# Eleven 512-column matmuls of a live operand with ones between the products of the up and the down projection of a hybrid decoder layer

## The chip, the cores and the metric

The kernel runs on one core of one Trainium2 chip. The metric is the device time of one execution in microseconds, the median of several runs. Beside it there is one execution taken by the hardware profiler; every row of a view comes from that one.

## The reference, cut to what matters

One decoder layer, float32, 512 tokens of 2048 channels. It has an adaptive normalisation, two attention branches with gates, and then a feed-forward part with a causal three-tap convolution:

```python
x = x + gt_a * parallel_mixers(h, ...)
h = rms_norm(x, g_ffn[l]) * (1.0 + sc_f) + sh_f
x = x + gt_f * conv_ffn(h, w_up[l], w_conv[l], b_conv[l], w_down[l])

def conv_ffn(h, w_up, w_conv, b_conv, w_down):
    u = h @ w_up                                    # 512 x 2048 by 2048 x 11264
    up = jnp.pad(u, ((0, 0), (CONV_W - 1, 0), (0, 0)))
    conv = b_conv
    for j in range(CONV_W):
        conv = conv + w_conv[j] * up[:, j:j + S]
    gate, val = jnp.split(conv, 2, axis=-1)         # 5632 each
    return (jax.nn.silu(gate) * val) @ w_down       # 5632 x 2048
```

The change touches only the two matrix products of `conv_ffn`.

## The kernel before, in words

Every float32 product is made of three matmuls: each operand is split into a high part (a rounded copy, made by ScalarE) and a low part (the rest, made by VectorE), and high·high, high·low and low·high are accumulated in PSUM. Weights arrive by DMA on SyncE's queue in the tile `raw` and are split into `whl`; activations lie in `slot` tiles of 128 x 512.

Before the feed-forward part, most matmuls have 512 columns (`mm3`, lines 188 to 190). The last of these, in `up_group(0)`, make the first 8 column tiles of the up projection and end at about 1321.5 us of the profiled execution.

The rest of the up projection and all of the down projection go through `seven`. It takes a list of `Pair`s. A pair makes two 128-row output tiles (for all 512 tokens) from a 2 x 2 block product done with seven block products in place of eight (a Strassen-like scheme): `p1, p7, p6, p2, p5, p4, p3`, each with its own evacuation `e1 ... e3`. One block product is `K` contraction tiles by three matmuls of 256 columns (lines 1256 to 1258). It goes to X (the left half of the pair's first bank `bx`), Y or Z (the halves of its second bank `by`). Four bank pairs go round (`all_banks`), so pair n uses the banks that pair n-4 used. The second bank of a pair is first written by `p7`, its second product, and is read last in `e4`, after its sixth.

`work_up` has 40 pairs with K = 8 (168 matmuls each; the tile of the gate half and of the value half of `w_up`). `work` has 32 pairs in four chunks c of 8, with K = `DH[c]` = 5, 6, 6, 5 (105, 126, 126 and 105 matmuls a pair). The chunks add into `x1_d`, and the last one writes the output.

`run` goes through the products in order. For each it first prepares the weights of the product `AHEAD` further on: VectorE makes sums and differences of weight blocks in place (`comb`, line 1133), and `hilo` splits the result (line 175 on ScalarE, 176 on VectorE; `tc.issue_after(left[0].ins)` keeps that split behind the last evacuation). Then it issues the product's matmuls and its evacuation (`copy`, lines 1137 and 1139, ScalarE; `plus`, lines 1143 and 1145, VectorE). A hook per product does side work: in the up projection it makes early sums, in the down projection it loads (line 1754) and splits the operands of the next chunk. Those operands, made from the f tiles in DRAM, are kept in `held_by[c]` until the chunk's last pair. `h2[0][0]` is the high part of the first contraction tile of h; it is an operand of all 40 up pairs.

The order on each engine is that of the program, sorted by priorities and a planner's estimated times, with `issue_after` where it is set by hand.

Two lines elsewhere put 512-column matmuls with the all-ones tile `ones_r` as weights into the stream. They are in `flush_cols`, which spreads sums over the partitions, and fall now and then between the 256-column matmuls of an earlier use of `seven` (the gate columns, 583 to 743 us):

```python
PE.matmul(b, ones_r, hi, start=True, stop=False)    # line 937
PE.matmul(b, ones_r, lo, start=False, stop=True)    # line 938
```

Of the kernel before, what the change touches and what calls it, by code (L numbers as in the profile page):

```python
# [21 lines left out]
KD = D // P  # L22
# [9 lines left out]
def trunk_layer_kernel(  # L32
# [21 lines left out]
    DH=(5, 6, 6, 5),  # L54
# [6 lines left out]
    V, A, G, PE, SP = nc.vector, nc.scalar, nc.gpsimd, nc.tensor, nc.sync  # L61
# [14 lines left out]
    def get(dt=F32):  # L76

        i = min(free, key=lambda n: rested[n])
        free.remove(i)
        if cur[i] is None or cur[i].dtype != dt:  # L80
            cur[i] = pool.tile([P, T], dt, name=f"slot{i}", tag=f"slot{i}")
        held[id(cur[i])] = i
        return cur[i]
# [4 lines left out]
    def put(*ts, lag=2):  # L88

        for t in ts:  # L90
            i = held.pop(id(t))
            rested[i] = clock[0] + lag
            free.append(i)
# [4 lines left out]
    ones_r = pool.tile([P, P], F32R, name="ones_r")  # L98
# [46 lines left out]
    last = {}  # L145
# [767 lines left out]
    done = [0]  # L913
# [167 lines left out]
    KH = KD // 2  # L1081
# [8 lines left out]
    def operands(act, ts):  # L1090
        return (quarter(act, 0, 0), quarter(act, KH, 0), quarter(act, KH, HT)) + tuple(sums(ts, n) for n in range(4))
# [8 lines left out]
    class Pair:  # L1100


        def __init__(self, rs, load, fin, K=KH, scale=None, onto=None):
            self.rs, self.load, self.fin, self.K, self.scale, self.onto = rs, load, fin, K, scale, onto

    def seven(work, pairs_of_banks, hook=None, AHEAD=2, ring=None):

# [129 lines left out]
        def prepare(q):  # L1237
            if q < len(steps):
                ready[q] = steps[q][0]()
# [5 lines left out]
        def run(then=None):  # L1245
            for q, (_, o, r, ev, first, K) in enumerate(steps):
                prepare(q + AHEAD)
                if then:
                    then(q - len(steps))
                wh, wl = ready.pop(q)  # L1250
                assert len(r) == K
                for k in range(K):
                    ks = slice(k * P, (k + 1) * P)
                    rh, rl = r[k]
                    last = k == K - 1
                    PE.matmul(o, wh[:, ks], rh, start=first and k == 0, stop=False, skip_group_check=True)  # L1256
                    PE.matmul(o, wh[:, ks], rl, start=False, stop=False, skip_group_check=True)  # L1257
                    PE.matmul(o, wl[:, ks], rh, start=False, stop=last, skip_group_check=True)  # L1258
                ev()
                clock[0] += 1  # L1260
                if hook:
                    hook(q, len(steps))
# [7 lines left out]
    for i in range(KH // 2):  # L1270
        raw = [get() for _ in range(4)]
        ta, tb_ = get(), get()
        for j in range(2):
            k, o = 2 * i + j, slice(j * HT, (j + 1) * HT)
# [10 lines left out]
    def gate_out(i):  # L1285
        def fin(u1, u2):
            G.dma_start(gate_d[G0 + 2 * i], u1)
            G.dma_start(gate_d[G0 + 2 * i + 1], u2)
            put(u1, u2)
        return fin  # L1290
# [10 lines left out]
    def gate_hook(q, n):  # L1301
        gate_tick()
        if q == n - 7:
            reload_mq()

    rs = operands(h, h_sums)
    start, run = seven([Pair(rs, lambda blk, i=i: w_gs[i, blk], gate_out(i)) for i in range((31 - G0) // 2)],
          ((MM[0], MM[1]), (MM[2], MM[3])), gate_hook)
# [257 lines left out]
    h2 = []  # L1566
# [3 lines left out]
    for tb in range(4):  # L1570
        spread = PE.matmul(rb[:, tb * P:(tb + 1) * P], rstd2[:, tb:tb + 1].to_broadcast([P, P]), ident,
                           start=True, stop=True)
# [27 lines left out]
    NF_ = DFF // P  # L1600
# [3 lines left out]
    KINDS = ("r11", "t3", "t2", "r21", "t1", "t4", "r22")  # L1604
# [74 lines left out]
    def f_tile(i, u1, u2, give):  # L1679
        j = 4 + i  # L1680
        g = conv(j, u1)
        A.activation(g, g, AF.Silu)
        v = conv(44 + j, u2)
        give((u1, u2))
        V.tensor_tensor(v, v, g, ALU.mult)
        f_out(j, v)
        put(g)
# [4 lines left out]
    def ffn_out(i):  # L1692
        def fin(u1, u2):
            for n, ds, _ in late:
                if n == i:
                    G.dma_start(ds[0], u1)
                    G.dma_start(ds[1], u2)
                    ring.extend((u1, u2))
                    return
            f_tile(i, u1, u2, ring.extend)  # L1700
        return fin
# [41 lines left out]
    held_by = [{n: [] for n in KINDS} for _ in DH]  # L1743
# [69 lines left out]

    all_banks = [(bank[2 * i], bank[2 * i + 1]) for i in range(4)]
    rs = operands(h2, tsum)
    work_up = [Pair(rs, lambda blk, i=i: w_ups[i, blk], ffn_out(i)) for i in range(NF_ - 4)]

    def down_pair(c, j):
        ns = (2 * j, 2 * j + 1)
        x1 = []  # L1820

        def load(blk):
            if c == len(DH) - 1 and not x1:
                for n in ns:
                    x1.append(get())
                    G.dma_start(x1[-1], x1_d[n])
            return w_downs[c][j, blk]

        def fin(*us):
            for i, (n, u) in enumerate(zip(ns, us)):  # L1830
                if x1:
                    V.tensor_tensor(u, u, x1[i], ALU.add)
                    G.dma_start(out[n * P:(n + 1) * P, :], u)
                else:
                    G.dma_start(x1_d[n], u, accum_op=ALU.add)
            ring.extend(us)
            put(*x1)

        o = ops[c]
        return Pair(tuple(o[n] for n in ("r11", "r21", "r22", "t1", "t2", "t3", "t4")), load, fin, K=DH[c],  # L1840
                    scale=tuple(mod[:, 80 + n:81 + n] for n in ns),
                    onto=(lambda i: (out[ns[i] * P:(ns[i] + 1) * P, :], x1[i]))
                    if c == len(DH) - 1 and j == KD // 2 - 1 else None)

    ring = deque(get() for _ in range(4))
    up_start, up_run = seven(work_up, all_banks, up_hook, ring=ring)
    work = [down_pair(c, j) for c in range(len(DH)) for j in range(KD // 2)]

    def hook(q, n):
        c, r = divmod(q, 56)  # L1850
        if r >= 49:
            put(*held_by[c][KINDS[r - 49]])
        ahead(q + 1, c + 1)
        late_tiles(q)
# [73 lines left out]
```

## Time and profile before

| | |
|---|---|
| three runs | 2515.29, 2515.98, 2541.91 us; median 2515.98 |
| profiled execution, its own time | 2519.35 us |
| its span, first to last instruction | 2517.3 us |
| granted TensorE clock over the span | 0.999 |
| busy: TensorE matmul / VectorE / ScalarE / GpSimd | 99% / 86% / 51% / 15% |

The profiled execution has 2.05 us outside its span, and is 3.4 us above the median of the runs.

In the views, PE is a TensorE matmul, PEld a weight load, DVE VectorE, ACT ScalarE, POOL GpSimd, SP SyncE. Matmuls overlap in the pipeline, and their ends are modelled: a 256-column matmul is shown as 276 ns long though the next one starts earlier. So the time that a matmul takes from the stream is the distance from its start to the next start, not its duration. A view by windows counts each instruction that touches the window. In a row of the timeline the columns are start (us), duration (us), engine, line, operation, output<-input, shapes, count and, in brackets, the idle time before it and what ended it.

### The profile page before, as it was taken

How to read it: one execution, taken by the hardware profiler on the slowest of the kernel's cores; microseconds unless marked ns; L12 is line 12 of the kernel's file. 1: busy time of each engine (PE TensorE's matmuls, PEld its weight loads, DVE VectorE, ACT ScalarE, POOL GpSimd, SP SyncE). 2: the span in 40 equal slices, each digit the busy share in tenths (PEclk: the TensorE clock that was granted, in tenths of full speed). 3: DMA queues.
4: the chain of work that ended last, by engine and by line, in shares of the span. 5: the costliest groups of instructions: out<-in, count | busy, mean ns of one | idle time of the engine just before them, and what ended most of it. 6: DMA issues, size and time to landing. Idle time of an engine off the chain costs nothing.

```text
span 2517.3 us, 45148 instructions
## 1 busy us (share of the span) xinstructions
PE 2500.6 (99%) x17328; PEld 2281.1 (91%) x17328; DVE 2168.0 (86%) x3484; ACT 1283.2 (51%) x2039; POOL 374.1 (15%) x671
## 2 busy tenths in 40 slices
PE   9999999999999999999999999999999999999999
PEld 8887688889998778888889999999999999999999
DVE  6976997788878767977879999999999998989988
ACT  6564444444445445323445555555555555666654
POOL 1000011110023224200101000000011024414120
PEclk9999999999999999999999999999999999999999
DMA  9953146555685479976524343343344458878673
GB/s 363 390 156 98 49 146 191 180 164 180 202 275 172 147 233 349 304 266 211 190 76 153 124 150 130 126 154 129 127 153 151 131 170 235 233 170 233 164 210 124
DMA packets 216444, 466.41 MB, mean 185 GB/s; under 512 B 23930, under 2 KB 65556, under 8 KB 216228
## 3 DMA queue, kind: packets, MB, share of 16 engines
q1 hardware_dynamic: 170404, 344.93, 42.1%
q0 software_dynamic: 45792, 118.59, 15.5%
q8 instruction: 135, 2.21, 0.4%
q14 instruction: 81, 0.66, 0.1%
q10 hardware_dynamic: 32, 0.01, 0.0%
HBM read 398.16 MB, written 65.27 MB: 184 GB/s over the span
## 4 chain that ended last, share of the span: by engine, by line
PE 80%; issue 10%; DMA 4%; DVE 3%; POOL 1%; ACT 1%; SPq 0%; POOLq 0%; DVEq 0%; ACTq 0%
PE bank L1256 16%; PE bank L1258 16%; PE bank L1257 15%; PE bank L188 8%; PE bank L189 8%; PE bank L190 8%; PE bank L419 2%; DMA slot<-in_w_ada 2%; PE bank L420 2%; PE bank L421 2%; DMA raw<-in_w_ada 1%; PE bank L655 1%; PE bank L1404 1%; DMA slot<-f 1%; PE bank L844 1%
## 5 line engine op out<-in xcount | busy, mean ns | idle before, releaser
L1256 PE MATMUL bank<-slot,whl 128*128 128x256 f32 x3920 | 1080.7, 277 | 4.9 <-ACT slot L1137 2.3
L1257 PE MATMUL bank<-slot,whl 128*128 128x256 f32 x3920 | 1079.2, 276 | 0.0
L1258 PE MATMUL bank<-slot,whl 128*128 128x256 f32 x3920 | 1068.8, 277 | 1.9 <-DVE whl L176 1.8
L1256 PEld LDWEIGHTS bank<-slot,whl 128*128 128x128 f32 x3920 | 735.8, 188 | 8.1 <-ACT slot L1137 3.7
L1257 PEld LDWEIGHTS bank<-slot,whl 128*128 128x128 f32 x3920 | 735.9, 188 | 0.2
L1258 PEld LDWEIGHTS bank<-slot,whl 128*128 128x128 f32 x3920 | 729.8, 188 | 2.9 <-DVE whl L176 2.9
L175 ACT ACTIVATE whl<-raw 128x1024 fp32r<-128x1024 f32 (+2 forms) x560 | 531.4, 950 | 349.8 <-PE bank L1257 177.3
L176 DVE TENSOR_TENSOR whl<-raw,whl 128x1024 fp32r<-128x1024 f32 (+2 forms) x560 | 607.9, 1088 | 86.7 <-ACT whl L175 83.6
L1133 DVE TENSOR_TENSOR raw<-raw 128x1024 f32<-128x1024 f32 (+2 forms) x320 | 347.6, 1086 | 5.4 <-DMA raw<-in_w_ups 3.1
L167 ACT ACTIVATE whl<-raw 128x1024 fp32r<-128x1024 f32 (+4 forms) x182 | 187.4, 1034 | 294.7 <-PE bank L190 152.9
L168 DVE TENSOR_TENSOR whl<-raw,whl 128x1024 fp32r<-128x1024 f32 (+4 forms) x182 | 216.3, 1190 | 88.5 <-ACT whl L167 86.4
L189 PE MATMUL bank<-slot,whl 128*128 128x512 f32 x592 | 234.9, 397 | 0.0
L188 PE MATMUL bank<-slot,whl 128*128 128x512 f32 x592 | 232.2, 400 | 0.7 <-ACT slot L1586 0.7
L188 PE MATMUL bank<-whl,slot 128*128 128x512 f32 (+2 forms) x608 | 230.6, 382 | 0.7 <-DVE slot L1368 0.7
L190 PE MATMUL bank<-whl,slot 128*128 128x512 f32 (+2 forms) x608 | 230.8, 380 | 0.0
L189 PE MATMUL bank<-whl,slot 128*128 128x512 f32 (+2 forms) x608 | 230.3, 379 | 0.0
L190 PE MATMUL bank<-slot,whl 128*128 128x512 f32 x592 | 229.9, 397 | 0.0
L889 DVE SCALAR_TENSOR_TENSOR slot<-slot,c_act,slot 128x512 f32<-128x512 f32 x203 | 151.4, 748 | 23.8 <-DMA slot<-in_w_ada 22.0
L1139 ACT ACTIVATE slot<-bank 128x256 f32<-128x256 f32 x192 | 73.5, 383 | 174.8 <-PE bank L1258 174.6
L188 PEld LDWEIGHTS bank<-whl,slot 128*128 128x128 f32 x608 | 114.1, 188 | 22.6 <-issue 2.8
L188 PEld LDWEIGHTS bank<-slot,whl 128*128 128x128 f32 x592 | 111.2, 188 | 25.4 <-issue 1.7
L189 PEld LDWEIGHTS bank<-slot,whl 128*128 128x128 f32 x592 | 111.3, 188 | 24.3 <-issue 1.2
(315 smaller groups left out, 3165.0 us busy)
## 6 DMA issues: line engine op xcount, KB each, us to landing
slot<-in_w_ada SPq DMA_DIRECT2D x344, 256.0 KB, 5.0
raw<-in_w_ups SPq DMA_DIRECT2D x160, 512.0 KB, 3.6
raw<-in_w_in SPq DMA_DIRECT2D x50, 512.0 KB, 3.5
raw<-in_w_down SPq DMA_DIRECT2D x64, 384.0 KB, 4.3
raw<-in_w_down SPq DMA_DIRECT2D x64, 320.0 KB, 4.5
slot<-f POOLq DMA_DIRECT2D x154, 128.0 KB, 4.9
f<-slot POOLq DMA_DIRECT2D x66, 256.0 KB, 5.3
raw<-in_w_gs SPq DMA_DIRECT2D x32, 512.0 KB, 4.2
```

The lines of the kernel that those rows point to most:

```text
L167: A.activation(hi, raw[:, :w], AF.Copy)
L168: last["lo"] = V.tensor_tensor(lo, raw[:, :w], r32(hi), ALU.subtract)
L175: return (A.activation(dst_hi, src, AF.Copy), V.tensor_tensor(dst_lo, src, r32(dst_hi), ALU.subtract))
L176: V.tensor_tensor(dst_lo, src, r32(dst_hi), ALU.subtract))
L188: PE.matmul(o, lh, rh, start=first, stop=False)
L189: PE.matmul(o, lh, rl, start=False, stop=False)
L190: PE.matmul(o, ll, rh, start=False, stop=last)
L889: V.scalar_tensor_tensor(acc, ts[i], c_act[:, k:k + 1], acc, op0=ALU.mult, op1=ALU.add)
L1133: V.tensor_tensor(o[:, :W], a[:, :W], b[:, :W], op)
L1256: PE.matmul(o, wh[:, ks], rh, start=first and k == 0, stop=False, skip_group_check=True)
L1257: PE.matmul(o, wh[:, ks], rl, start=False, stop=False, skip_group_check=True)
L1258: PE.matmul(o, wl[:, ks], rh, start=False, stop=last, skip_group_check=True)
```

## The change

`Pair` takes one more argument, `wide`. Where a pair has it, `run` issues one more matmul ahead of the pair's first product: weights `ones_r` (128 x 128 ones), moving operand a 128 x 512 high-part tile that is live at that time, output the whole second bank of the pair, which holds nothing needed then; `p7` starts it anew later. Nothing reads the result. It is pinned behind the last matmul of the product before. Pairs 2, 4 and 20 of the up projection have it (operand `h2[0][0]`), and pairs 1 and 5 of each of the four chunks of the down projection (operand: the first tile kept for the chunk): 3 + 8 = 11.

```diff
-        def __init__(self, rs, load, fin, K=KH, scale=None, onto=None):
+        def __init__(self, rs, load, fin, K=KH, scale=None, onto=None, wide=None):
...
                 wh, wl = ready.pop(q)
                 assert len(r) == K
+                if q % 7 == 0 and work[q // 7].wide:
+                    with tc.issue_after(done.ins):
+                        PE.matmul(pairs_of_banks[q // 7 % len(pairs_of_banks)][1], ones_r, work[q // 7].wide(), start=True, stop=True)
...
-                    PE.matmul(o, wl[:, ks], rh, start=False, stop=last, skip_group_check=True)
+                    done = PE.matmul(o, wl[:, ks], rh, start=False, stop=last, skip_group_check=True)
...
-    work_up = [Pair(rs, lambda blk, i=i: w_ups[i, blk], ffn_out(i)) for i in range(NF_ - 4)]
+    work_up = [Pair(rs, lambda blk, i=i: w_ups[i, blk], ffn_out(i), wide=(lambda: h2[0][0]) if i in (2, 4, 20) else None)
+               for i in range(NF_ - 4)]
...
-                    if c == len(DH) - 1 and j == KD // 2 - 1 else None)
+                    if c == len(DH) - 1 and j == KD // 2 - 1 else None,
+                    wide=(lambda: held_by[c][KINDS[0]][0]) if j in (1, 5) else None)
```

More of the change, by code (lines that the diff above doesn't have):

```diff
@@ L1100, in trunk_layer_kernel @@
     class Pair:
-        def __init__(self, rs, load, fin, K=KH, scale=None, onto=None):
-            self.rs, self.load, self.fin, self.K, self.scale, self.onto = rs, load, fin, K, scale, onto
+        def __init__(self, rs, load, fin, K=KH, scale=None, onto=None, wide=None):
+            self.rs, self.load, self.fin, self.K, self.scale, self.onto, self.wide = rs, load, fin, K, scale, onto, wide
     def seven(work, pairs_of_banks, hook=None, AHEAD=2, ring=None):
```

## Prediction

> **What bounds the kernel now.** I read the page first: busy shares, clock, chain and the costliest groups.
>
> ```profile
> span 2517.3 us, 45148 instructions
> PE 2500.6 (99%) x17328; PEld 2281.1 (91%) x17328; DVE 2168.0 (86%) x3484; ACT 1283.2 (51%) x2039; POOL 374.1 (15%) x671
> ...
> PEclk9999999999999999999999999999999999999999
> ...
> PE 80%; issue 10%; DMA 4%; DVE 3%; POOL 1%; ACT 1%; SPq 0%; POOLq 0%; DVEq 0%; ACTq 0%
> ...
> L1256 PE MATMUL bank<-slot,whl 128*128 128x256 f32 x3920 | 1080.7, 277 | 4.9 <-ACT slot L1137 2.3
> ```
>
> TensorE is busy throughout and makes 80% of the chain that ended last. The time is that of its stream of matmuls, so anything added to the stream counts unless it falls into a wait.
>
> Next, the stages of the changed part by windows on PE. The matmul counts give the limits: 40 up pairs of 168, then chunks of 8 pairs of 105, 126, 126 and 105. (A count runs one or two over, for instructions that only touch the window.)
>
> ```profile
> core 0: us, PE busy (x), PEclk, DMA share, GB/s
> 1321.54:2084.85 763.31, 762.59 (x6721) 1.00 0.43 144
> 2084.85:2184.71 99.86, 97.34 (x842) 1.00 0.80 216
> 2184.71:2304.02 119.31, 118.36 (x1010) 1.00 0.75 202
> 2304.02:2418.75 114.73, 114.65 (x1010) 1.00 0.76 197
> 2418.75:2514.20 95.45, 95.38 (x842) 1.00 0.47 155
> ```
>
> Chunks 1 and 2 do the same work, but chunk 1 takes 4.6 us longer; chunk 0 takes 4.4 us longer than chunk 3. To see why, I put windows without any wait side by side (same columns).
>
> ```profile
> 1340.00:1425.00 85.00, 85.00 (x752) 1.00 0.42 140
> 2205.00:2290.00 85.00, 85.00 (x724) 1.00 0.65 166
> 638.00:651.00 13.00, 13.00 (x113) 1.00 0.58 189
> 655.00:668.00 13.00, 13.00 (x117) 1.00 0.60 207
> ```
>
> All are fully busy at granted clock 1.00, and yet there are **two paces** of the same 256-column matmul. The last one juts out of the window by up to 0.28 us, so 85.28/752 = 113.4 ns and 85.28/724 = 117.8 ns. The difference, 4.4 ns, lasts as long as nothing interrupts the stream. The slow pace begins here at a wait and ends at another:
>
> ```profile
> 2203.04 0.28 PE L1258 MATMUL bank<-slot,whl 128*128 128x256 f32 x1
> 2203.83 0.39 PE L1256 MATMUL bank<-slot,whl 128*128 128x256 f32 x1 [0.51 <-ACT slot L1137]
> 2204.05 0.28 PE L1257 MATMUL bank<-slot,whl 128*128 128x256 f32 x1
> ...
> 2292.85 0.28 PE L1258 MATMUL bank<-slot,whl 128*128 128x256 f32 x1
> 2293.57 0.39 PE L1256 MATMUL bank<-slot,whl 128*128 128x256 f32 x1 [0.43 <-ACT whl L175]
> ```
>
> So 88.8 us at 117.8 ns, 754 matmuls, cost 754 x 4.4 ns = 3.3 us; that is most of chunk 1's excess. Chunk 0's excess is waits.
>
> The other runs matter here. 2541.91 is 26 us above its neighbours. The up projection has next to no waits (762.59 busy of 763.31, and 6720 x 113.4 ns is 762.0), so a pace once taken can last through it; at the slow one its 6,720 matmuls would cost 30 us more. That fits, but no row shows that run.
>
> **The change part by part.** It adds eleven matmuls of 512 columns with weights `ones_r`, and removes or moves nothing. VectorE, ScalarE, GpSimd and the DMA queues issue nothing new. The trace has this very operation between products: `flush_cols` in the gate columns.
>
> ```profile
> 651.35 0.28 PE L1257 MATMUL bank<-slot,whl 128*128 128x256 f32 x1
> 651.47 0.39 PE L937 MATMUL bank<-slot,ones_r 128*128 128x512 f32 x1
> 651.70 0.28 PE L1258 MATMUL bank<-slot,whl 128*128 128x256 f32 x1
> 651.81 0.28 PE L1256 MATMUL bank<-slot,whl 128*128 128x256 f32 x1
> 651.93 0.28 PE L1257 MATMUL bank<-slot,whl 128*128 128x256 f32 x1
> ...
> 654.08 0.28 PE L1258 MATMUL bank<-slot,whl 128*128 128x256 f32 x1
> 654.19 0.40 PE L938 MATMUL bank<-slot,ones_r 128*128 128x512 f32 x1
> 654.43 0.28 PE L1256 MATMUL bank<-slot,whl 128*128 128x256 f32 x1
> 654.55 0.28 PE L1257 MATMUL bank<-slot,whl 128*128 128x256 f32 x1
> 654.67 0.28 PE L1258 MATMUL bank<-slot,whl 128*128 128x256 f32 x1
> 654.78 0.28 PE L1256 MATMUL bank<-slot,whl 128*128 128x256 f32 x1
> 654.89 0.28 PE L1257 MATMUL bank<-slot,whl 128*128 128x256 f32 x1
> ```
>
> *Price in the quick pace.* From 654.08 to 654.89, 0.81 us, there are five 256-column steps at 113.4 ns, 0.567; the rest, **0.24 us**, is the wide one with the slight irregularity behind it. Its weights load beside the matmul before, as with every other.
>
> *Effect on the pace.* The window 638 to 651 ran at 13.28/113 = 117.5 ns, and 655 to 668 at 13.28/117 = 113.5 ns; the switch is at the wide matmul at 651.47. The one at 654.19 came in the quick pace and left it so. A wide matmul between products thus ends the slow pace, and I think this is what the change would do if it does anything.
>
> The sum, against the profiled execution's 2519.35 us:
> - *Up projection, pairs 2, 4 and 20* (a pair is 168 x 113.4 ns = 19.05 us, so about 1361, 1399 and 1704 us): no wait absorbs them there; 3 x 0.24 = +0.72.
> - *Down, chunk 2 pair 5, chunk 3 pairs 1 and 5*: these chunks run almost without a wait; with chunk 2 pair 1, which is near the last small one, 4 x 0.24 = +0.96.
> - *Chunk 0 pairs 1 and 5, chunk 1 pair 1*: waits of PE follow within a pair or two:
>
> ```profile
> PE bank L1256 <- ACT slot L1137: 2.3, 4, 0.8
> PE bank L1256 <- ACT whl L175: 1.0, 3, 0.4
> ```
>
>  These (2084 to 2320 us) are for ScalarE's split of a weight block or the evacuation ahead of it. If their end is set by ScalarE and VectorE, the added time falls into them: between 0 and 3 x 0.24 = 0.72. I take 0, since the waits total 3.3 us.
> - *Chunk 1 pair 5* (about 2259): +0.24, and it ends the slow pace 34 us before 2292.85: 34/0.1178 = 288 matmuls x 4.4 ns = -1.27. The wait at 2292.85 may take that back: -1.0 to +0.24.
>
> Sum: 0.72 + 0.96 + (0 to 0.72) + (-1.0 to +0.24) = +0.7 to +2.6 us. The profiled execution is 3.4 us above the median of the runs, about one slow stretch. So I take it that the median run has no such stretch, hence no gain in chunk 1 (and its pair 5 goes into the wait at 2293 like its pair 1), and get 2515.98 + 1.7 = **2517.7 us**. With the ends it is 2516.7 to 2518.6.
>
> *Waits added.* The wide matmul needs its bank read out, by the pair four earlier, three pairs ago: 57 us in the up projection, 36 us in the shorter chunks. Only pair 2 follows other work; the last read of those banks is
>
> ```profile
> L1597 DVE SCALAR_TENSOR_TENSOR slot<-bank,wcv,slot x4: 741/745/745, 1320.3 to 1329.4; 128x510 f32<-128x510 f32 x4
> ```
>
>  and ends at 1330.2, 31 us before. The operands were read by an earlier pair. If it did wait, everything on PE would stand behind it, one for one.
>
> A place where the Trainium skill speaks against the change: "TensorE: Matmul & The Clock Gate", section "Back-to-back issue gap", gives a warm gap of N/2.4 + 2.5 ns, which is 109 ns at 256 columns and 216 at 512. By that page there is one pace only, nothing to switch, and the eleven cost an estimated 2.4 us in full. The trace agrees on neither figure: 113.4 and 117.8 ns at granted clock 1.00, and 0.24 us for the wide one.
>
> **Rivals.**
>
> *A slow stretch is cured.* If usual runs do have slow stretches like that in chunk 1, and waits don't take the time back, up to 3.3 us go for 1.7 spent: 2514.4. For it: 2204 to 2292 recurs if the waits there are the same each time. Against: pair 1 of chunk 1 comes just ahead of that wait, so the nearest cure comes 55 us after it.
>
> *The wide matmul leaves PE in the slow pace* (slower). Behind a run of 512-column matmuls the stream did start slow:
>
> ```profile
> 1321.32 0.39 PE L190 MATMUL bank<-slot,whl 128*128 128x512 f32 x1
> 1321.55 0.28 PE L1256 MATMUL bank<-slot,whl 128*128 128x256 f32 x1
> 1321.66 0.28 PE L1257 MATMUL bank<-slot,whl 128*128 128x256 f32 x1
> 1321.78 0.28 PE L1258 MATMUL bank<-slot,whl 128*128 128x256 f32 x1
> 1321.90 0.28 PE L1256 MATMUL bank<-slot,whl 128*128 128x256 f32 x1
> ```
>
>  Three steps in 0.35 us are 117 ns. If one lone wide matmul did this too, all of the up projection from 1361 on (724 us, 6,380 matmuls, 28 us) and chunks 2 and 3 from 2318 (196 us, 1,730, 7.6 us) would be slow: 2515.98 + 2.6 + 35.6 = 2554. If only that at pair 20 did, (2085 - 1704)/0.1134 x 4.4 ns = 14.8: 2532. It decides at the first one, at 1361. Against it: both insertions above ended in the quick pace.
>
> *The order shifts.* Eleven more instructions change the planner's times, and splits or evacuations on ScalarE and VectorE can come in another order in chunks 0 to 2. The waits of 3.3 us go or double, and a wait may start a slow stretch of 3.3 us: 2511 to 2524.
>
> *It does nothing that counts*: all eleven lie in waits or are dropped: 2516.0. Against it: there are no waits at seven of the places.
>
> **How the numbers follow.** Forecast 0.58, a cured stretch 0.13, slow pace left behind 0.08, order shifted 0.16, nothing 0.05. The range is 2511 to 2526: it takes the forecast, the cure, nothing and the shifted order, with 2 us above for a slow stretch in more than one place; it leaves out the slow pace left behind. A measurement of this kernel tells a difference of about 1%, 25 us, from no change. No case reaches 25 us below (0.02 for what I don't see); above it are the slow pace in full and a start in it that no wide matmul ends (0.06); same 0.92.
>
> **What the profile after would show.** Eleven matmuls of 128x512 at a new line in `run`, none with idle time before it, each 0.24 us to the next start. 1340 to 1425 has 752 matmuls less some three; a window from 1710 to 2080 keeps 113.4 ns. Chunk 2 and 3 are 0.5 us longer each, chunk 0 and 1 may be shorter or longer by their waits. If the pace is 113.4 ns in every window behind a wide matmul, the reading of the pace is right. If a window after one is at 117.8 ns, it is wrong, and so is the price. If a run like that of 2541.91 starts the up projection slow, the wide matmul at 1361 ends it, and the run costs at most 336 matmuls x 4.4 ns = 1.5 us more: the runs after should lie closer together. A forecast 10 us off would mean that the order of the splits has moved: seen as new waits of PE for lines 175, 176 or 1137 in the up projection, where there are none now.

## The result, and the profile after

Twenty-two runs each: the kernel after has a median of 2519.06 us (2514.37 to 2527.11), the kernel before 2542.95 us (2513.21 to 2549.70). The ratio of the mean times is 0.9942, 95% interval 0.9915 to 0.9969: about half a per cent faster; the medians lie 24 us apart, 0.9%. (Single runs of 3,000 us and more, two of before and three of the kernels tried further below, are left out throughout.)

The medians hide what happened. The times of before fall into **two groups**, 8 of 22 at 2513 to 2519 us (median 2515.6) and 14 of 22 at 2542 to 2550 us (median 2544.3), with nothing between. After has one group. Against the lower group of before it is 3.4 us slower; against the upper it is 25 us faster. The three times shown beforehand had two of the lower group, so 2515.98 was not the typical time. No run of the upper group of before was profiled; what such a run looks like is seen below in other kernels.

The profiled execution of after took 2518.64 us, span 2516.5 us. Its stages by windows on PE (duration, PE busy and matmul count, clock, DMA share, GB/s), in the order up projection, chunks 0 to 3:

```profile
1319.71:2083.77 764.06, 763.34 (x6724) 1.00 0.43 143
2083.77:2185.11 101.34, 99.22 (x844) 1.00 0.80 213
2185.11:2302.25 117.14, 116.11 (x1012) 1.00 0.78 208
2302.25:2417.47 115.22, 115.14 (x1012) 1.00 0.75 196
2417.47:2513.40 95.93, 95.86 (x844) 1.00 0.47 154
```

The up projection is 0.75 us longer than in the execution of before that was profiled (one of the lower group), and chunks 2 and 3 are 0.5 us longer each: three matmuls and twice two, at 0.25 us. Chunk 1, whose long slow stretch is gone, is 2.2 us shorter; chunk 0 is 1.5 us longer. Little is gained against *that* execution. The line of the added matmuls, and the first of them in the timeline:

```profile
L1254 PE MATMUL bank<-slot,ones_r x11: 393/396/398, 1359.7 to 2478.9; 128*128 128x512 f32 x11
```

```profile
1359.62 0.28 PE L1261 MATMUL bank<-slot,whl 128*128 128x256 f32 x1
1359.74 0.40 PE L1254 MATMUL bank<-slot,ones_r 128*128 128x512 f32 x1
1359.97 0.28 PE L1261 MATMUL bank<-slot,whl 128*128 128x256 f32 x1
1360.09 0.28 PE L1259 MATMUL bank<-slot,whl 128*128 128x256 f32 x1
1360.21 0.28 PE L1260 MATMUL bank<-slot,whl 128*128 128x256 f32 x1
1360.32 0.28 PE L1261 MATMUL bank<-slot,whl 128*128 128x256 f32 x1
1360.44 0.28 PE L1259 MATMUL bank<-slot,whl 128*128 128x256 f32 x1
```

From 1359.62 to 1360.44 there are five ordinary steps (0.567 us) in 0.82: the wide one costs 0.25 us. No row has idle time in front of it, and none of the eleven has. The pace by windows:

```profile
1340.00:1425.00 85.00, 85.00 (x750) 1.00 0.42 140
1710.00:2080.00 370.00, 370.00 (x3267) 1.00 0.44 148
2154.00:2174.00 20.00, 20.00 (x172) 1.00 0.63 159
2205.00:2290.00 85.00, 85.00 (x750) 1.00 0.70 174
```

The long window behind pair 20 has 370.28/3267 = 113.3 ns: quick. In chunk 0 a slow stretch remains (20.28/172 = 117.9 ns), behind waits that follow the wide matmul of pair 5. That matmul, at 2148.82, had itself ended a slow stretch of 87 matmuls (from 2138.57), but a wait 1.6 us later began the next one. The waits of PE in chunks 0 and 1 are much as before, 2.9 us in place of 3.3:

```profile
PE bank L1259 <- ACT slot L1137: 1.8, 3, 0.8
PE bank L1259 <- ACT whl L175: 1.1, 3, 0.5
```

### The profile page after: what moved, and what is told of

The parts are those of the page before. It is cut to its first block, busy times and chain, and to the rows that moved or that the text cites. A ratio compares the mean times of both kernels' runs of the same rounds, so it can differ in the third digit from the quotient of the medians.

```text
span 2516.5 us, 45172 instructions
## 1 busy us (share of the span) xinstructions
PE 2499.6 (99%) x17339; PEld 2280.0 (91%) x17339; DVE 2167.6 (86%) x3484; ACT 1282.4 (51%) x2039; POOL 374.3 (15%) x671
## 4 chain that ended last, share of the span: by engine, by line
PE 78%; issue 11%; DMA 5%; DVE 4%; POOL 1%; ACT 1%; SPq 0%; POOLq 0%; DVEq 0%; ACTq 0%
PE bank L1259 15%; PE bank L1261 15%; PE bank L1260 15%; PE bank L188 8%; PE bank L189 8%; PE bank L190 8%; PE bank L419 2%; PE bank L420 2%; PE bank L421 2%; DMA slot<-in_w_ada 2%; DMA raw<-in_w_ada 1%; PE bank L655 1%; DVE slot L889 1%; PE bank L1407 1%; DMA slot<-f 1%
## 5 line engine op out<-in xcount | busy, mean ns | idle before, releaser
L176 DVE TENSOR_TENSOR whl<-raw,whl 128x1024 fp32r<-128x1024 f32 (+2 forms) x560 | 608.2, 1089 | 87.0 <-ACT whl L175 84.1
```

The source lines that it names most:

```text
L176: V.tensor_tensor(dst_lo, src, r32(dst_hi), ALU.subtract))
```

## The experiments

Each kernel is the one after with one edit. All were run twelve times, in four sets, each beside 17 to 35 runs of before, which again fall into two groups: 19 of 35, 21 of 34, 15 of 29 and 13 of 17 in the lower one. The share of the groups moves the median of before between 2517 and 2543, so the groups are read below, more than the ratios.

**Where is the gain: up or down projection?**

```diff
# up2_only
-    ... wide=(lambda: h2[0][0]) if i in (2, 4, 20) else None)
+    ... wide=(lambda: h2[0][0]) if i in (2,) else None)
-                    wide=(lambda: held_by[c][KINDS[0]][0]) if j in (1, 5) else None)
+                    (never)
# down8_only: (2, 4, 20) -> (), the eight of the down projection stay
# up20_only: (2, 4, 20) -> (20,), none in the down projection
```

> Only the wide matmul at pair 2 of the up projection is kept; the other ten are left out. Theory (two paces): before has two kinds of run, 8 of 22 at 2513 to 2519 us and 14 of 22 at 2542 to 2550, because the waits at the start of the up projection leave its stream of 256-column matmuls at 113.4 or at 117.8 ns; one wide matmul at 1361 us ends the slow pace for the rest of the up projection. So all runs lie at 2514 to 2522, none at 2540 or above, and the median is 2516 to 2519. Rival (the gain is made in the down projection, by its wide matmuls or by the instructions whose order moved there): two kinds of run as before, median near 2543.

Measured: 2512.32 to 2521.16, median 2515.71, one group; ratio 0.9943 (0.9904 to 0.9982). The whole gain with one matmul, as the theory said: no run is in the upper group. Its profile also shows the cure, for in this run the waits at 1323 to 1335 us had left the slow pace:

```profile
1338.00:1357.00 19.00, 19.00 (x163) 1.00 0.43 147
1360.00:1379.00 19.00, 19.00 (x170) 1.00 0.49 175
1700.00:2080.00 380.00, 380.00 (x3356) 1.00 0.45 149
```

The wide matmul stands at 1357.36. Ahead of it the step is 19.28/163 = 118.3 ns, behind it 19.28/170 = 113.4 ns, and at the end of the stage 380.28/3356 = 113.3 ns.

> The eight wide matmuls of the down projection are kept, the three of the up projection are left out. Theory (two paces, the up projection decides): two kinds of run again, 2515 to 2522 and 2542 to 2552, about two thirds in the upper group; if the profiled run is of the upper kind, a window 1340 to 1425 us holds 724 matmuls in place of 752. Rival (gain in the down projection): one kind of run, 2515 to 2522.

Measured: 5 runs at 2517.55 to 2519.97, 6 at 2545.79 to 2550.06. Two groups, as the theory said: the eight of the down projection cure nothing that counts, and put both groups up: by their medians, 2519.2 and 2547.3 against 2515.8 and 2545.9 for before in the same set. The profiled run is of the upper group, the first view of such a one:

```profile
1335.00:1365.00 30.00, 30.00 (x267) 1.00 0.41 143
1370.00:1430.00 60.00, 60.00 (x512) 1.00 0.45 146
1700.00:2080.00 380.00, 380.00 (x3229) 1.00 0.40 133
```

Quick to 1365 (30.28/267 = 113.4 ns), slow from 1370 (60.28/512 = 117.7 ns) to the end of the stage (380.28/3229 = 117.8 ns), at a granted clock of 1.00 in every row. Between them is this (timeline of the same kernel):

```profile
1366.32 0.28 PE L1259 MATMUL bank<-slot,whl 128*128 128x256 f32 x1
1366.43 0.28 PE L1260 MATMUL bank<-slot,whl 128*128 128x256 f32 x1
...
1366.60 0.19 PEld L1261 LDWEIGHTS bank<-slot,whl 128*128 128x128 f32 x1
1366.61 0.38 PE L1261 MATMUL bank<-slot,whl 128*128 128x256 f32 x1
...
1366.83 0.28 PE L1259 MATMUL bank<-slot,whl 128*128 128x256 f32 x1
```

The step from 1366.43 is 0.18 us in place of 0.11. The weight load of that matmul starts 0.17 us after the matmul before it, where the others start within 0.01 us; in the trace it waits for VectorE, whose split of the low part of the weights (L176) ended at 1366.55. **A wait of 0.06 us starts a slow pace that lasts to the wait at 2116.36, (2116.4 - 1366.8)/0.1178 = 6,363 matmuls, and costs 6,363 x 4.4 ns = 28 us.** No view of waits lists it. Not every late step does this: in the profile of up2_only, four of 0.14 to 0.18 us (2136 to 2186 us) left the pace quick. The expectation had such a run slow from before 1340; a run can also turn slow here.

> Only the wide matmul at pair 20 of the up projection is kept. Theory (two paces; the wide matmul ends the slow one where it stands): of the 29 us that a slow run loses, those up to 1704 us are still lost: (1704 - 1335)/0.1134 = 3254 matmuls x 4.4 ns = 14 us. So two kinds of run, about 2516 and 2531, none at 2542 or above. Rival (a wide matmul acts only near the start, or by what it does to the first waits): two kinds of run, 2516 and 2544. Rival (the pace is a property of the run and not of the place): the same 2516 and 2544, or all at 2516.

Measured: 7 runs at 2515.09 to 2521.30, 5 at 2529.28 to 2533.53 (four of them 2529.28 to 2529.38), none at 2540. The profiled run is a quick one, so the upper group is read from its times alone. If such a run is slow from 1367 to the wide matmul and quick behind it, that is 335/0.1133 = 2,957 matmuls (the wide one stands at 1702 in the quick run), 13.0 us; 2515.7 + 13.0 = 2528.7. That fits the four at 2529.3: the wide matmul acts where it stands, on the pace that it finds.

**Does it protect against later waits?**

```diff
# up1_only: if i in (1,); up0_only: if i in (0,); none in the down projection
# up0_only besides: no pin for the very first product
```

> One wide matmul, at pair 1 of the up projection (about 1342 us): behind the waits of PE at 1322 to 1333, but ahead of 1366, where the profiled slow run of the kernel with the eight of the down projection alone took up its slow pace at a wait of 0.06 us. Theory (a wait can set the pace, a wide matmul ends the slow one only where it stands): a run that waits at 1366 is slow to the end of the up projection all the same, unless the 0.24 us that the wide matmul adds also cover that wait. If they don't: two kinds of run, 2516 and 2543. If they do: one kind, 2513 to 2522. Rival (a wide matmul protects the stream from later waits): one kind of run, and its trace has waits of PE behind 1342 us that leave the pace at 113.4 ns.

Measured: eleven runs at 2513.37 to 2525.65, one at 2538.24; median 2516.23. Eleven runs are quick. Whether they had no wait behind 1342 us, or the added 0.24 us covered it, their times do not tell. The wide matmul does not protect: the run at 2538 is the profiled one, and it was quick behind its wide matmul and turned slow at a later wait:

```profile
1340.00:1390.00 50.00, 50.00 (x443) 1.00 0.50 168
1395.00:1445.00 50.00, 50.00 (x427) 1.00 0.39 130
```

```profile
1391.51 0.28 PE L1260 MATMUL bank<-slot,whl 128*128 128x256 f32 x1
1391.62 0.35 PE L1259 MATMUL bank<-slot,whl 128*128 128x256 f32 x1
1391.81 0.28 PE L1260 MATMUL bank<-slot,whl 128*128 128x256 f32 x1
```

50.28/443 = 113.5 ns, then 50.28/427 = 117.7 ns, with a step of 0.19 us between; here too the trace has a weight load waiting for VectorE (L1145, which ended at 1391.53). A wide matmul at pair 4, at 1399, would catch such a run.

> One wide matmul, at pair 0, the very start of the up projection (1321 us), ahead of all its waits (about 1322, 1328, 1332 us). Theory (the last wait or wide matmul sets the pace): it changes nothing that lasts, because three waits follow: two kinds of run, 2513 to 2521 and 2541 to 2550, as before. Rival (once set quick at the start of the projection the stream stays so): one kind, 2513 to 2521, median 2516.

Measured: 6 runs at 2512.55 to 2520.23 and 6 at 2543.21 to 2546.49, as the theory said. Ahead of the waits a wide matmul is of no use; the profiled run is slow from 1338 on:

```profile
1700.00:2080.00 380.00, 380.00 (x3229) 1.00 0.42 133
```

**What of the matmul does it: its length, or the ones?** Five kernels with the same eleven places.

```diff
# eleven_256: 256 columns
-  PE.matmul(pairs_of_banks[...][1], ones_r, work[q // 7].wide(), start=True, stop=True)
+  PE.matmul(pairs_of_banks[...][1][:, :HT], ones_r, work[q // 7].wide()[:, :HT], start=True, stop=True)
# eleven_384, eleven_128: [:, :3 * P], [:, :P]
# eleven_256_wh, eleven_512_wh: wh[:, 0:P] (the next product's first block) for ones_r
```

> The same eleven matmuls at the same places, with 256 columns in place of 512. Theory (it is the irregular length that moves the phase between weight loads and streaming): a matmul as long as its neighbours leaves the pace as it was, so two kinds of run as before, 2515 to 2522 and 2542 to 2552, each about 11 x 0.11 = 1.2 us above those of before. Rival (any matmul with other operands put in ends the slow pace): one kind of run, 2515 to 2521.

Measured: 2553.15 to 2563.48, one group, median 2556.89; both expectations were wrong. The pace breaks at the first inserted matmul, at 1359.57, and is slow to the end:

```profile
1335.00:1359.00 24.00, 24.00 (x215) 1.00 0.37 129
1362.00:1386.00 24.00, 24.00 (x206) 1.00 0.44 146
1720.00:2080.00 360.00, 360.00 (x3059) 1.00 0.41 133
```

(24.28/215 = 112.9, 24.28/206 = 117.9, 360.28/3059 = 117.8 ns.) One matmul as long as its neighbours, with other weights, costs the rest of the projection.

> The same eleven places, 256 columns, but with the next product's first weight block in place of the ones as weights. The kernel with 256 columns and ones was always slow from its first inserted matmul on (2553 to 2563). Theory A (what cost the pace there is the tile of ones as weights, whose load comes in a few ns late): with ordinary weights the inserted matmul is one more like its neighbours and leaves the pace alone: two kinds of run, about 2517 and 2545. Theory B (any matmul of 256 columns put in there, for its moving operand or its bank, costs the pace): always slow, 2553 to 2563.

Measured: 6 runs at 2516.96 to 2518.63, 6 at 2543.09 to 2550.31: theory A, as to the times. With ordinary weights the inserted 256-column matmul leaves the pace as it finds it; in the profiled run it was quick, 360.28/3179 = 113.3 ns. These are the same instructions at the same places as in eleven_256, so it is not their order that makes the difference. The reason that the theory gave does not show: in the trace of eleven_256 the load of the first ones starts 4 ns after the matmul before, like the others. The windows of eleven_256_wh:

```profile
1362.00:1386.00 24.00, 24.00 (x214) 1.00 0.48 160
1720.00:2080.00 360.00, 360.00 (x3179) 1.00 0.45 146
```

> The same eleven matmuls with ones, of 384 columns. Theory (a matmul longer than the load of the weights gives that load time to get ahead again, and so the quick pace): as with 512 columns, one kind of run, 2514 to 2522, about 11 x 0.06 = 0.6 us below the kernel with 512. Rival (512, the whole bank, is special): slow always, as with 256 columns, 2552 to 2563.

Measured: one group, 2516.65 to 2524.39, median 2519.91; the theory's group, though not below the kernel after.

> The same eleven places with ones, 128 columns. Theory (a matmul shorter than its weight load gives that load no time to get ahead): always slow from the first on, as with 256 columns and ones: 2552 to 2563. Rival (any length that differs from the neighbours' moves the stream out of the slow pace): one kind of run, 2514 to 2521.

Measured: one group at a new place, 2535.07 to 2542.87, median 2539.65. Neither expectation. The windows between pairs 2, 4 and 20 tell why:

```profile
1335.00:1360.00 25.00, 25.00 (x223) 1.00 0.39 131
1362.00:1398.00 36.00, 36.00 (x308) 1.00 0.44 155
1402.00:1702.00 300.00, 300.00 (x2649) 1.00 0.42 137
1710.00:2080.00 370.00, 370.00 (x3144) 1.00 0.42 138
```

113.4, 117.8, 113.4, 117.8 ns: each inserted matmul **turned** the pace over, from quick to slow as well as back.

> The eleven matmuls of 512 columns with the next product's first weight block in place of the ones. Theory (the length does it, not the ones): one kind of run, 2514 to 2523 as with ones, none above 2535. Rival (the ones have a part in ending the slow pace, as they had in starting it at 256 columns): two kinds of run, about 2518 and 2546.

Measured: one group, 2536.13 to 2543.82, median 2541.71; ratio 1.0069 (1.0033 to 1.0105). Not the theory, and the rival only in that the ones do have a part. It too turns the pace over; this run came to pair 2 slow:

```profile
1335.00:1358.00 23.00, 23.00 (x198) 1.00 0.36 121
1362.00:1396.00 34.00, 34.00 (x302) 1.00 0.47 152
1400.00:1710.00 310.00, 310.00 (x2634) 1.00 0.40 132
1720.00:2080.00 360.00, 360.00 (x3179) 1.00 0.44 144
```

117.6, 113.5, 117.8, 113.3 ns. So 512 or 384 columns with ones end in the quick pace from either, in every instance of these profiles that no wait follows at once; the other combinations do not.

**A version with less.**

```diff
# up2_up4: if i in (2, 4); none in the down projection
# up2_up4_down2: besides, if (c, j) in ((0, 6), (1, 2))
```

> Wide matmuls of 512 columns at pairs 2 and 4 of the up projection alone. Theory (what they cure lies in the up projection: slow paces begun by waits up to about 1391 us): one kind of run, 2512 to 2521, none above 2530, median 2515 to 2517; 9 x 0.24 = 2.2 us at most below the kernel after, whose median was 2519. Rival (the eight in the down projection pay for themselves, by ending slow stretches there): median 2518 to 2521.

Measured: 2513.10 to 2521.16, median 2517.02; ratio 0.9962 (0.9928 to 0.9997). One group.

> Pairs 2 and 4 of the up projection, and in the down projection only pair 6 of chunk 0 and pair 2 of chunk 1, each behind a wait after which profiled runs went slow (2138 and 2204 us). Theory: such a stretch costs 1 to 3.3 us where it occurs, so the median is 0 to 2 us below that with pairs 2 and 4 alone, and the upper end of the runs lower. Rival (waits at the end of those stretches take the time back): no difference, or 0.5 us more for the two matmuls.

Measured: ten runs at 2513.30 to 2522.21, median 2517.4, ratio 0.9945 (0.9902 to 0.9988). No gain over pairs 2 and 4 alone; the rival holds within what ten runs can tell. In its profile both wide matmuls of the down projection came upon the quick pace (113.4 and 113.5 ns ahead of them), so it shows no cure there, and a slow stretch follows a later wait, 2178 to 2203.

Pairs 2 and 4 alone, or pair 2 alone at 2515.71, have lower medians than the kernel after (2519.06) by 2 and 3 us. Each had its own set of runs: above the lower group of before in the same set, the three stand 0.8, 0.0 and 3.4 us. That is the size of the 9 or 10 matmuls saved (0.24 each), but they were not timed against each other, and the median of that lower group itself lay between 2515.6 and 2518.6 in the five sets. Pair 4 is cheap cover for a run like that of up1_only.

## Why the prediction was right or wrong, by its steps

- *Two paces at granted clock 1.00, 4.4 ns apart, that last until something interrupts.* Right: 113.3 and 117.8 ns in every kernel that was profiled.
- *A wide matmul with ones ends the slow pace and keeps the quick one.* Right, shown by the profile of up2_only and the groups of up2_only and up20_only. As the prediction put it ("A wide matmul between products", any such) it was too broad: with other weights or lengths it turns the pace over or spoils it.
- *0.24 us each, no wait added.* Right: 0.25 us, no idle time in front of any.
- *The step that failed: "So I take it that the median run has no such stretch".* With it the sum was added to 2515.98, the time of a run that is quick in the up projection. The cost of a slow one was worked out (30 us, beside the run of 2541.91), and that a wide matmul would end it, but this got no term in the sum and no chance of its own: two of three runs were quick, and I took that for the rule. Of 22 runs 14 were slow. The gain of the change is the cure of those, 2544.3 - 2515.6 = 28.7 us each, less its own price. So the time after came out near the forecast (2519.06 for 2517.7), since all its runs are quick, while the change was forecast as 1.7 us slower and the median fell by 24.
- *A slow stretch is cured.* This rival had the right mechanism with the wrong stretch: chunk 1 for 3.3 us in place of the up projection for 29. The stretch in chunk 1 is no rule either: in the five profiled kernels without a wide matmul there (up2_only, up20_only, up1_only, up0_only, up2_up4) the 754 matmuls behind that wait went at 113.3 or 113.4 ns. In up2_only (83.28/734 = 113.5 by the window):

```profile
2202.00:2285.00 83.00, 83.00 (x734) 1.00 0.68 174
```

- *The cost against a quick run, +0.7 to +2.6.* After stands 3.4 us above the lower group of before; 2.6 of it is the eleven at 0.24. The rest was not settled; slow stretches in chunk 0 like that at 2154 are one candidate.
- *Waits in chunks 0 and 1 hide three of them.* Open: chunk 0 took 1.5 us more and chunk 1 2.2 us less, with slow stretches of their own in one execution each.
- *The wide matmul leaves the slow pace (2532 to 2554).* Not for 512 columns with ones. For 256 with ones it is just what happened: 2557.
- *The order shifts.* The waits of PE in chunks 0 and 1 hardly changed (2.9 us for 3.3), up2_only has the gain without the down projection's matmuls, and eleven_256_wh, with a matmul at all eleven places, has two groups as before.
- *The runs lie closer together.* Right, and it was the main effect: 13 us in place of 36.
- The rule of the Trainium skill that was weighed ("TensorE: Matmul & The Clock Gate", section "Back-to-back issue gap") is one that the section itself calls the gap of a single matmul in isolation; for a stream with weight loads it has another figure, about 131 ns at 512 columns, which the prediction left out. No run agrees with either: the same 256-column matmuls went at 113.3 and 117.8 ns, the difference decided the result, and the 512-column stream ahead of the up projection in the profile of before went at 226.7 ns (1310 to 1321 us).

## What to carry to other kernels

Where a kernel is one uninterrupted stream of matmuls, count matmuls per window and compare the pace between places and runs; busy share, waits and granted clock showed nothing here, and a wait of 0.06 us cost 28 us. If a few runs of the same kernel fall into two groups, the sum has to be made for both and weighted by more runs than three. A cheap matmul of the right form behind the last wait can set the pace, but its form has to be tried: of six forms only two ended in the quick pace from both.

## What the runs showed of the hardware that was not expected

The pace of the 256-column float32 stream depends on how it was last disturbed. What an inserted matmul did to it, by the profiles (the first row is that of the change; pace ahead of the matmul and behind it, up to the next wait):

| inserted | found quick | found slow |
|---|---|---|
| 512, ones | stays quick | becomes quick |
| 384, ones | stays quick | becomes quick (seen once) |
| 256, ones | becomes slow | stays slow |
| 128, ones | becomes slow | becomes quick |
| 256, ordinary weights | stays quick | stays slow (seen once) |
| 512, ordinary weights | becomes slow | becomes quick (one of seven stayed slow) |

The weights matter, though all are 128 x 128 blocks of the same type; `ones_r` differs from the others in its values and in its place, and no run tells these apart. The trace keeps nanoseconds, and they show where the 4.4 ns lie. In the execution of before, a matmul starts 110.0 ns after its weight load in the quick window (1340 to 1425 us) and 114.4 ns after it in the slow one (2205 to 2290), while the next load starts 3.3 ns after the matmul in both. Why this distance has two values, which of them a wait leaves, and why the tile of ones acts otherwise stay open: ones copied to another address, or ordinary weights in a tile of their own, would be the next thing to try, and were not tried.
